# Products ordered by weight tile: all high parts of a tile first, then all its low parts

## The chip, the cores and the metric

The kernel runs on one core of a Trainium2 chip. The metric is the device time of one execution in microseconds; a time stands for the median of several runs. PE is TensorE, DVE is VectorE, ACT is ScalarE, POOL is GpSimd and SP is SyncE, which issues the weight transfers. PEld is TensorE loading the stationary operand of a product, which it does beside the products.

## The reference

A decoder trunk of two layers on a sequence of 256 rows and 1024 channels, in float32. In each layer:

```
h = rmsnorm(x);  p = h @ w_in                      # 1024 x 5888
y_a = short_conv(...) @ w_a_out                    # three mixers on parts of p
y_b = (silu(g) * retention(q, k, v)) @ w_b_out
y_c = spatial_gating(gelu(z)) @ w_c_out
x += (g_a*y_a + g_b*y_b + g_c*y_c) @ w_o           # g_*: sigmoid gates from p
x += cross_attention(rmsnorm(x), rmsnorm(mem))     # xa_q, xa_k, xa_v, xa_o
h = rmsnorm(x)
x += (silu(h @ w1) * (h @ w3)) @ w2                # 1024 -> 2816 -> 1024
```

## The kernel before

**Splitting.** Every float32 weight and activation is split into a high part (rounded to the matmul's float32r) and a low part (the rest). A product of two such numbers is taken as high x high + high x low + low x high.

**The weight stream.** All weights lie in one stream of 128x1024 tiles in the order of use, 320 tiles. `fetch` loads one tile (`raw`, five buffers, an SP DMA), ACT copies it to `hi` (L106), and DVE subtracts to get `lo` (L67), four buffers each. `weights(cols)` hands out the next columns of the current tile.

**Four kinds of chunk.** `chunk_T` makes a transposed result of 256 output channels: for each k of 128 input channels it takes 256 columns of weights; each half of 128 columns is the stationary operand of a 512-column product (`hi` with both parts of x) and of a 256-column product (`lo` with the high part of x). One k is thus two pairs of a 512 and a 256, a chunk of eight k has 32 products, and a tile feeds four k. `chunk_N` (z, g, attention values xv) has the activations stationary and 512 or 256 weight columns moving: for each block of 128 rows high x `hi`, low x `hi`, high x `lo`. `chunk_pair` does two such chunks (qk and v) side by side, one weight tile per k: twelve products of 512. `chunk_y` (branch outputs y, and the last two chunks of w2) multiplies 256 columns each time. The names in the trace are those of the result tiles: gt (gates, 12 chunks a layer), f (w1 and w3, 22 chunks), w (w2), wo, k, q, xv, xo (attention), ax, ac, ab (convolution inputs), and s, pT, av, o, sc, vm, qkT, rT, suT for small products between.

**What sets the order.** TensorE's instructions stand in the order of the program: `InOrder` chains them. The other engines' order is made by the framework's scheduler from a simulated timeline, so it can change when TensorE's order does; each engine then works strictly in its order.

**Accumulators.** `chunk_T`, `chunk_N` and `chunk_pair` share two PSUM buffers (tag mm), so a chunk can begin only when the one two before it has been read: by `summed` (an ACT copy L190 and a DVE add, written `ev<-...`), by `residual` (two DVE adds, `xT<-...`), or by ACT copies (for qk, L331, `mixb<-qk`). Hooks place small products (norm sums, scores, transposes) ahead of a certain k inside a chunk.

In the gates of each layer the memory rows `m` are loaded, scaled on POOL and split by ACT and DVE into `mmt` (lines 454 to 464).

Of the kernel before, what the change touches and what calls it, by code (L numbers as in the profile page):

```python
# [11 lines left out]
F32 = mybir.dt.float32  # L12
# [5 lines left out]
P = 128  # L18
# [3 lines left out]
KT = D // P  # L22
# [3 lines left out]
TW = 1024  # L26
# [28 lines left out]
def decoder_trunk(ctx: ExitStack, tc: tile.TileContext, a, out):  # L55
    nc = tc.nc
    V, A, G, T = nc.vector, nc.scalar, nc.gpsimd, InOrder(tc, nc.tensor)
# [5 lines left out]
    psm = ctx.enter_context(tc.tile_pool(name="psm", bufs=2, space=bass.MemoryType.PSUM))  # L63
# [25 lines left out]
    state = dict(pos=0, loaded=0)  # L89
# [3 lines left out]
    def fetch():  # L93
        n = state["loaded"]
        if n == tiles:
            return
        state["loaded"] = n + 1
        raw = wts.tile([P, TW], F32, tag="raw", name=f"raw{n}", bufs=5)
        hi = wts.tile([P, TW], F32R, tag="hi", name=f"hi{n}", bufs=4)
        lo = wts.tile([P, TW], F32R, tag="lo", name=f"lo{n}", bufs=4)  # L100
        for at, c, m in pieces[n]:
            nc.sync.dma_start(raw[:, at:at + m], ws[c // TW, :, c % TW:c % TW + m])
        w = TW if n else TW // 2
        for c in range(0, TW, w):
            sl = slice(c, c + w)
            A.activation(hi[:, sl], raw[:, sl], AF.Copy)  # L106
            tt(V, lo[:, sl], raw[:, sl], f32(hi[:, sl]), ALU.subtract)
        if n >= 4 and later:
            later.pop(0)()
        ready.append((hi, lo))  # L110

    def weights(cols):
        pos = state["pos"]
        while state["loaded"] <= min(pos // TW + AHEAD, tiles - 1):
            fetch()
        o = pos % TW
        state["pos"] = pos + cols
        hi, lo = ready[pos // TW]
        return hi[:, o:o + cols], lo[:, o:o + cols]


    def chunk_T(xs, kt, name, hooks=None, ps=None, ks=None):


        if ps is None:
            ps = psm.tile([P, 2, 2, S], F32, tag="mm", name=name)
        for k in ks or range(kt):
            if hooks and k in hooks:
                hooks[k]()
            wh, wl = weights(2 * P)  # L130
            x = xs(k)
            for i in range(2):
                c = slice(i * P, (i + 1) * P)
                T.matmul(ps[:, i].rearrange("p t s -> p (t s)"), wh[:, c], x.rearrange("p t s -> p (t s)"),
                         start=(k == 0), stop=False, skip_group_check=True)
                T.matmul(ps[:, i, 1], wl[:, c], x[:, 0], start=False, stop=(k == kt - 1), skip_group_check=True)
        return ps

    def chunk_N(xs, name, hooks=None, n=512):

        ps = psm.tile([P, 2, 512], F32, tag="mm", name=name)
        for k in range(KT):
            if hooks and k in hooks:
                hooks[k]()
            wh, wl = weights(n)
            x = xs(k)
            for b in range(2):
                sl = slice(b * P, (b + 1) * P)
                T.matmul(ps[:, b, 0:n], x[:, 0, sl], wh, start=(k == 0), stop=False)
                T.matmul(ps[:, b, 0:n], x[:, 1, sl], wh, start=False, stop=False)  # L150
                T.matmul(ps[:, b, 0:n], x[:, 0, sl], wl, start=False, stop=(k == KT - 1))
        return ps[:, :, 0:n]

    def chunk_pair(xs, names, hooks):

        pair = [psm.tile([P, 2, 512], F32, tag="mm", name=name) for name in names]
        for k in range(KT):
            if k in hooks:
                hooks[k]()
            x = xs(k)  # L160
            for ps in pair:
                wh, wl = weights(512)
                for b in range(2):
                    sl = slice(b * P, (b + 1) * P)
                    T.matmul(ps[:, b], x[:, 0, sl], wh, start=(k == 0), stop=False)
                    T.matmul(ps[:, b], x[:, 1, sl], wh, start=False, stop=False)
                    T.matmul(ps[:, b], x[:, 0, sl], wl, start=False, stop=(k == KT - 1))
        return pair

    def chunk_y(xs, kt, name, n=2):  # L170

        ps = pss.tile([P, 2, S], F32, tag="sm", name=name)
        for k in range(kt):
            wh, wl = weights(n * P)
            x = xs(k)
            for i in range(n):
                c = slice(i * P, (i + 1) * P)
                T.matmul(ps[:, i], wh[:, c], x[:, 0], start=(k == 0 and i == 0), stop=False, skip_group_check=True)
                T.matmul(ps[:, i], wh[:, c], x[:, 1], start=False, stop=False, skip_group_check=True)
                T.matmul(ps[:, i], wl[:, c], x[:, 0], start=False, stop=(k == kt - 1 and i == n - 1),  # L180
                         skip_group_check=True)
        return ps

    def of(t, k0=0):
        return lambda k: t[:, k0 + k]

    def summed(ps):

        t = wrk.tile([P, 2, S], F32, tag="ev", name="ev", bufs=4)
        A.activation(t, ps[:, :, 1], AF.Copy)  # L190
        tt(V, t, ps[:, :, 0], t, ALU.add)
        return t
# [13 lines left out]
    xs = res.tile([P, KT, 2, S], F32R, name="xs")  # L206
# [83 lines left out]
    def transposes(src, f, name):  # L290

        ps = pss.tile([P, 2, S], F32, tag="sm", name=f"{name}{f}")
        for i in range(2):
            for b in range(2):
                T.transpose(ps[:, i, b * P:(b + 1) * P], src[:, b, (f + i) * P:(f + i + 1) * P], ident)
        return ps
# [9 lines left out]
    for l in range(L):  # L306
# [5 lines left out]
        def pair(x):  # L312
            return x.rearrange("p b (h d) -> p b h d", h=8)
# [6 lines left out]
        def mix_rows():  # L320
            nrm["rb"] = rows_kept(nrm["rn"], f"rb_mix{l}")

        qk, vv = chunk_pair(of(xs), (f"qk{l}", f"v{l}"), {6: mix_cols, 7: mix_rows})
        rn, rb = nrm["rn"], nrm["rb"]
        r2 = wrk.tile([P, S], F32, tag="r2", name=f"r2{l}", bufs=1)
# [3 lines left out]
        t, ra, rbb = pair(mb[:, 0:2]), pair(mb[:, 2:4]), pair(mb[:, 4:6])  # L329
# [8 lines left out]
        for b in range(2):  # L338
            A.activation(vs[:, b], vv[:, b], AF.Copy, scale=rn[:, b:b + 1])

        zz = chunk_N(of(xs), f"z{l}")
        zt = mb[:, 8:10]
        for b in range(2):
# [17 lines left out]
        tt(G, vn, vn, mid(sgg[:, l], 2), ALU.mult)  # L361

        gg = chunk_N(of(xs), f"g{l}")
        sg = mm_[:, 5:7]
        for b in range(2):
# [5 lines left out]


        tx = summed(chunk_T(of(xs), KT, f"ax{l}"))


        scT = mm_[:, 2:5].rearrange("p i s -> p (i s)").rearrange("p (h s) -> p h s", h=4)
        for h in range(4):
            ps = pss.tile([P, 512], F32, tag="sm", name=f"sc{l}_{h}")
# [12 lines left out]
        for g in range(4):  # L391
            sl = slice(g * 64, (g + 1) * 64)
# [3 lines left out]
        G.memset(zp[:, :, 0:2], 0.0)  # L396
        tt(G, tx, tx, mid(r2, 2), ALU.mult)
        tc_ = summed(chunk_T(of(xs), KT, f"ac{l}"))
        tt(G, zp[:, :, 2:], tc_, tx, ALU.mult)
        yc = mb[:, 5].rearrange("p (i s) -> p i s", i=2)  # L400
# [12 lines left out]
        for b in range(2):  # L413
            ps = pss.tile([P, 512], F32, tag="sm", name=f"o{l}_{b}")
# [11 lines left out]
        for b in range(2):  # L426
            for h in range(4):
                i = 4 * b + h
# [3 lines left out]
            tt(G, rv, rv, sg[:, b], ALU.mult)  # L432

        tb = summed(chunk_T(of(xs), KT, f"ab{l}"))
        tt(G, tb, tb, mid(rb, 2), ALU.mult)
        tt(G, yc, yc, tb, ALU.mult)
# [5 lines left out]
        for c in range(12):  # L442
            t = summed(chunk_T(of(xs), KT, f"gt{l}_{c}"))
# [21 lines left out]
            if c == 1:  # L465
                for i in range(2):
                    ps = transposes(rr.rearrange("p b h d -> p b (h d)"), 2 * i, f"rT{l}")
# [6 lines left out]
        for c in range(4):  # L474
            ev = []
            for br, (k0, kn) in enumerate(((0, 2), (2, 4), (6, 2))):
                ps = chunk_y(of(mo, k0), kn, f"y{l}_{c}_{br}")
# [60 lines left out]
        def values(c, n, hooks):  # L538
            ps = chunk_N(of(mmt), f"xv{l}_{c}", hooks, n)
            A.activation(vt[:, :, 0, c:c + n], ps, AF.Copy)  # L540
            tt(V, vt[:, :, 1, c:c + n], ps, f32(vt[:, :, 0, c:c + n]), ALU.subtract)
# [32 lines left out]
        for j in range(4):  # L574
            if j < 2:
                ps = chunk_T(of(ox), KT, f"xo{l}_{j}", ps=xo[j], ks=range(4, KT))
            else:
                ps = chunk_T(of(ox), KT, f"xo{l}_{j}")
# [22 lines left out]
        hooks = {2: {0: ffn_cols}, 3: {0: ffn_rows}}  # L601
        ts = []
        part = [chunk_T(of(xs), KT, f"f{l}_{c}", ks=range(0, KT - 2)) for c in range(2)]
        for c in range(FT):
            if c < 2:
                ps = chunk_T(of(xs), KT, f"f{l}_{c}", ps=part[c], ks=range(KT - 2, KT))
            else:
                ps = chunk_T(of(xs), KT, f"f{l}_{c}", hooks=hooks.get(c))
# [20 lines left out]
    for n in (6, 7):  # L629
        ps = chunk_y(hidden, FT, f"w2_{n}", 1)  # L630
# [100 lines left out]
```

## Time and profile before

| | |
|---|---|
| median of three runs | 968.9 us (968.84 to 968.98) |
| the profiled execution | 969.4 us |
| its span, first to last instruction | 967.6 us |
| mean granted TensorE clock over the span | 0.995 |
| PE busy | 951.8 us (98%) |
| DVE, ACT busy | 713.7 us (74%), 539.8 us (56%) |

The profiled execution is 0.5 us above the median, and 1.8 us of it lie outside the span. Matmuls overlap, so PE being busy 98% of the span says only that it seldom stands still; how fast it goes is read from the starts of its products.

### The profile page before, as it was taken

How to read it: one execution, taken by the hardware profiler on the slowest of the kernel's cores; microseconds unless marked ns; L12 is line 12 of the kernel's file. 1: busy time of each engine (PE TensorE's matmuls, PEld its weight loads, DVE VectorE, ACT ScalarE, POOL GpSimd, SP SyncE). 2: the span in 40 equal slices, each digit the busy share in tenths (PEclk: the TensorE clock that was granted, in tenths of full speed). 3: DMA queues.
4: the chain of work that ended last, by engine and by line, in shares of the span. 5: the costliest groups of instructions: out<-in, count | busy, mean ns of one | idle time of the engine just before them, and what ended most of it. 6: DMA issues, size and time to landing. Idle time of an engine off the chain costs nothing.

```text
span 967.6 us, 14606 instructions
## 1 busy us (share of the span) xinstructions
PE 951.8 (98%) x5622; PEld 836.8 (86%) x5622; DVE 713.7 (74%) x884; ACT 539.8 (56%) x740; POOL 296.1 (31%) x232
## 2 busy tenths in 40 slices
PE   8999999999999999999999989999999999999996
PEld 6788889888998888888888878998889888888886
DVE  7679789886768866657655896799776778666654
ACT  6565765565645755654456465545665466656431
POOL 5943021320114644432134230024100345444211
PEclk9999999999999999999999999999999999999998
DMA  9664665555546565555656355555644556556541
GB/s 310 245 228 145 192 203 186 190 182 170 172 133 194 177 198 191 193 187 180 197 179 194 111 180 193 195 179 172 196 153 151 154 187 191 187 194 194 180 151 44
DMA packets 52630, 175.53 MB, mean 181 GB/s; under 512 B 6096, under 2 KB 6608, under 8 KB 52560
## 3 DMA queue, kind: packets, MB, share of 16 engines
q1 hardware_dynamic: 52128, 174.03, 55.9%
q8 instruction: 44, 0.72, 0.3%
q10 hardware_dynamic: 432, 0.57, 0.2%
q14 instruction: 26, 0.21, 0.1%
HBM read 173.53 MB, written 1.05 MB: 180 GB/s over the span
## 4 chain that ended last, share of the span: by engine, by line
PE 96%; DVE 2%; DMA 1%; issue 0%; SPq 0%; ACT 0%; DVEq 0%
PE f L43 25%; PE gt L43 14%; PE w L43 13%; PE y L43 5%; PE k L43 5%; PE xo L43 5%; PE wo L43 5%; PE xv L43 5%; PE q L43 5%; PE z L43 2%; PE g L43 2%; PE v L43 2%; PE qk L43 2%; PE av L43 1%; PE ac L43 1%; PE s L43 1%
## 5 line engine op out<-in xcount | busy, mean ns | idle before, releaser
L67 DVE TENSOR_TENSOR lo<-raw,hi 128x1024 fp32r<-128x1024 f32 (+1 forms) x321 | 436.8, 1363 | 200.0 <-ACT hi L106 198.0
L106 ACT ACTIVATE hi<-raw 128x1024 fp32r<-128x1024 f32 (+1 forms) x321 | 338.9, 1057 | 315.1 <-issue 67.5
L43 PE MATMUL f<-xs,hi 128*128 128x512 f32 x704 | 245.2, 393 | 0.0
L43 PE MATMUL f<-xs,lo 128*128 128x256 f32 x704 | 196.1, 279 | 0.0
L43 PEld LDWEIGHTS f<-xs,hi 128*128 128x128 f32 x704 | 131.9, 187 | 30.1 <-issue 0.4
L43 PE MATMUL gt<-xs,hi 128*128 128x512 f32 x384 | 136.5, 400 | 2.8 <-DVE ev L67 2.7
L43 PEld LDWEIGHTS f<-xs,lo 128*128 128x128 f32 x704 | 132.6, 188 | 0.0
L67 POOL TENSOR_TENSOR sq<-xT 128x512 f32<-128x512 f32 x27 | 45.8, 1695 | 239.3 <-DVE xT L67 234.5
L43 PE MATMUL gt<-xs,lo 128*128 128x256 f32 x384 | 107.8, 281 | 0.0
L67 POOL TENSOR_TENSOR ev<-ev,rb_ffn 128x512 f32<-128x512 f32 x44 | 63.8, 1453 | 108.3 <-DVE ev L67 85.3
L43 PEld LDWEIGHTS gt<-xs,hi 128*128 128x128 f32 x384 | 72.7, 189 | 20.6 <-DVE ev L67 4.0
L43 PEld LDWEIGHTS gt<-xs,lo 128*128 128x128 f32 x384 | 73.2, 191 | 0.0
L43 PE MATMUL w<-aB,hi 128*128 128x512 f32 (+1 forms) x198 | 62.7, 372 | 0.0
L43 PE MATMUL w<-aA,hi 128*128 128x512 f32 (+1 forms) x198 | 62.3, 371 | 0.0
L67 POOL TENSOR_TENSOR ev<-ev 128x256 f32<-128x256 f32 x44 | 50.5, 1151 | 20.1 <-ACT ev L597 20.1
L202 DVE SCALAR_TENSOR_TENSOR xs<-xT,par,xs 128x256 fp32r<-128x256 f32 x48 | 49.1, 1062 | 4.2 <-ACT xs L201 4.2
L43 PE MATMUL w<-aB,lo 128*128 128x256 f32 x176 | 49.5, 281 | 0.0
L43 PE MATMUL w<-aA,lo 128*128 128x256 f32 x176 | 49.4, 281 | 0.0
L43 PE MATMUL y<-mo,hi 128*128 128x256 f32 x256 | 46.1, 283 | 0.0
L43 PE MATMUL k<-mmt,hi 128*128 128x512 f32 x128 | 45.6, 400 | 0.0
L43 PE MATMUL q<-xs,hi 128*128 128x512 f32 x128 | 45.5, 398 | 0.0
L43 PE MATMUL xo<-ox,hi 128*128 128x512 f32 x128 | 45.4, 399 | 0.0
(251 smaller groups left out, 1779.9 us busy)
## 6 DMA issues: line engine op xcount, KB each, us to landing
raw<-in_ws SPq DMA_DIRECT2D x304, 512.0 KB, 3.5
raw<-in_ws SPq DMA_DIRECT2D x32, 256.0 KB, 4.0
m<-in_memT SPq DMA_DIRECT2D x12, 256.0 KB, 4.0
xT<-in_xT SPq DMA_DIRECT2D x4, 256.0 KB, 5.2
dec<-in_dec SPq DMA_DIRECT2D x1, 512.0 KB, 6.0
wm<-in_wsT SPq DMA_DIRECT2D x2, 256.0 KB, 4.8
out<-xT ACTq DMA_DIRECT2D x2, 256.0 KB, 2.3
sgg<-in_sgg SPq DMA_DIRECT2D x1, 256.0 KB, 5.1
```

The costliest lines, as they stand in the source:

```text
L43: ins = getattr(self.engine, name)(*args, **kwargs)
L67: e.tensor_tensor(o, x, y, op=op)
L106: A.activation(hi[:, sl], raw[:, sl], AF.Copy)
L202: V.scalar_tensor_tensor(lo, x, scale, f32(hi), ALU.mult, ALU.subtract)
```

## The change

Within each weight tile (or the part of it that lies between two hooks or chunk ends) all products with `hi` are issued first, and then all with `lo`. In `chunk_T` a full tile becomes eight products of 512 columns and then eight of 256, where the two alternated. In `chunk_pair` it becomes eight products with `hi` (qk four, v four) and four with `lo` (qk two, v two). The products, their operands, the number of weight loads and the weight stream stay. The core of the diff (`chunk_y` is changed in the same way):

```diff
+    def by_tile(ks, cols, hooks=None):
+        group = []
+        for k in ks:
+            hook = hooks.get(k) if hooks else None
+            if group and (hook or state["pos"] % TW == 0):
+                yield group
+                group = []
+            if hook:
+                hook()
+            group.append((k, *weights(cols)))
+        yield group
...
-        for k in ks or range(kt):
-            if hooks and k in hooks:
-                hooks[k]()
-            wh, wl = weights(2 * P)
-            x = xs(k)
-            for i in range(2):
-                c = slice(i * P, (i + 1) * P)
-                T.matmul(ps[:, i].rearrange("p t s -> p (t s)"), wh[:, c], x.rearrange("p t s -> p (t s)"),
-                         start=(k == 0), stop=False, skip_group_check=True)
-                T.matmul(ps[:, i, 1], wl[:, c], x[:, 0], start=False, stop=(k == kt - 1), skip_group_check=True)
+        for group in by_tile(ks or range(kt), 2 * P, hooks):
+            for k, wh, _ in group:
+                for i in range(2):
+                    T.matmul(ps[:, i].rearrange("p t s -> p (t s)"), wh[:, i * P:(i + 1) * P],
+                             xs(k).rearrange("p t s -> p (t s)"), start=(k == 0), stop=False, skip_group_check=True)
+            for k, _, wl in group:
+                for i in range(2):
+                    T.matmul(ps[:, i, 1], wl[:, i * P:(i + 1) * P], xs(k)[:, 0],
+                             start=False, stop=(k == kt - 1), skip_group_check=True)
...
+    def products_N(group, x):
+        blocks = [slice(b * P, (b + 1) * P) for b in range(2)]
+        for p, k, wh, _ in group:
+            for b in range(2):
+                T.matmul(p[:, b], x(k)[:, 0, blocks[b]], wh, start=(k == 0), stop=False)
+                T.matmul(p[:, b], x(k)[:, 1, blocks[b]], wh, start=False, stop=False)
+        for p, k, _, wl in group:
+            for b in range(2):
+                T.matmul(p[:, b], x(k)[:, 0, blocks[b]], wl, start=False, stop=(k == KT - 1))
...
-            for ps in pair:
-                wh, wl = weights(512)
-                for b in range(2):
-                    sl = slice(b * P, (b + 1) * P)
-                    T.matmul(ps[:, b], x[:, 0, sl], wh, start=(k == 0), stop=False)
-                    T.matmul(ps[:, b], x[:, 1, sl], wh, start=False, stop=False)
-                    T.matmul(ps[:, b], x[:, 0, sl], wl, start=False, stop=(k == KT - 1))
+            products_N([(ps, k, *weights(512)) for ps in pair], xs)
```

The change moves rows on the other engines too. On PE, at the end of the first layer's `chunk_pair` (the eighth k, tiles hi_281 and lo_282) and the beginning of z, stood:

```order
L43 MATMUL rb_mix_ps<-ident,rn_mix_273 128x128 x2
L43 MATMUL qk_172<-hi_281,xs 128x512 x2
L43 MATMUL qk_172<-lo_282,xs 128x512
L43 MATMUL qk_172<-hi_281,xs 128x512 x2
L43 MATMUL qk_172<-lo_282,xs 128x512
L43 MATMUL v_173<-hi_281,xs 128x512 x2
L43 MATMUL v_173<-lo_282,xs 128x512
L43 MATMUL v_173<-hi_281,xs 128x512 x2
L43 MATMUL v_173<-lo_282,xs 128x512
L43 MATMUL z_338<-hi_306,xs 128x512 x2
```

Now there stands, at the same place:

```order
L43 MATMUL rb_mix_ps<-ident,rn_mix_273 128x128 x2
L43 MATMUL qk_172<-hi_281,xs 128x512 x4
L43 MATMUL v_173<-hi_281,xs 128x512 x4
L43 MATMUL qk_172<-lo_282,xs 128x512 x2
L43 MATMUL v_173<-lo_282,xs 128x512 x2
L43 MATMUL z_338<-hi_306,xs 128x512 x8
```

The last product of qk moved from six places ahead of the end to two, and the first of v from the seventh place to the fifth.

On DVE, at the end of the first layer, `residual` of the last w2 chunk (w_3) stood with both its adds together, ahead of the first products of the second layer's v, which take its accumulator:

```order
L67 TENSOR_TENSOR lo_4691<-raw_4689,hi_4690 128x1024
L67 TENSOR_TENSOR lo_4710<-raw_4708,hi_4709 128x1024
L67 TENSOR_TENSOR xT<-w_3_4554,xT 128x512 x2
L67 TENSOR_TENSOR lo_4729<-raw_4727,hi_4728 128x1024
L202 SCALAR_TENSOR_TENSOR xs<-xT,par,xs 128x256 x2
```

Now:

```order
L67 TENSOR_TENSOR lo_4691<-raw_4689,hi_4690 128x1024
L67 TENSOR_TENSOR lo_4710<-raw_4708,hi_4709 128x1024
L67 TENSOR_TENSOR xT<-w_3_4554,xT 128x512
L67 TENSOR_TENSOR lo_4729<-raw_4727,hi_4728 128x1024
L67 TENSOR_TENSOR xT<-w_3_4554,xT 128x512
L214 SCALAR_TENSOR_TENSOR xs<-xT,par,xs 128x256 x2
```

The low part of a weight tile moved in between the two adds.

On DVE, in the second layer's retention (o_0 and o_1 are its outputs in PSUM, st, mv and rs the statistics, zp the convolution's input, mixb its result), from the statistics to the convolution, stood:

```order
L67 TENSOR_TENSOR lo_5251<-raw_5249,hi_5250 128x1024
L422 BN_STATS st_5181<-o_0_5184 128x6 x4
L67 TENSOR_TENSOR lo_5289<-raw_5287,hi_5288 128x1024
L423 BN_AGGR mv_5182<-st_5181 128x2 x2
L67 TENSOR_TENSOR ev<-ac_5126,ev 128x512
L423 BN_AGGR mv_5182<-st_5181 128x2 x2
L422 BN_STATS st_5181<-o_1_5197 128x6 x4
L423 BN_AGGR mv_5182<-st_5181 128x2 x4
L403 TENSOR_SCALAR mixb_4684<-zp,par 128x256 x2
L425 RECIPROCAL rs_5183<-rs_5183 128x8
L404 SCALAR_TENSOR_TENSOR mixb_4684<-zp,par,mixb_4684 128x256 x2
L429 TENSOR_SCALAR mixb_4684<-o_0_5184,mv_5182,rs_5183 128x128 x4
```

Now:

```order
L67 TENSOR_TENSOR lo_5289<-raw_5287,hi_5288 128x1024
L67 TENSOR_TENSOR ev<-ac_5126,ev 128x512
L434 BN_STATS st_5181<-o_0_5184 128x6 x4
L435 BN_AGGR mv_5182<-st_5181 128x2 x2
L434 BN_STATS st_5181<-o_1_5197 128x6 x2
L435 BN_AGGR mv_5182<-st_5181 128x2
L434 BN_STATS st_5181<-o_1_5197 128x6 x2
L435 BN_AGGR mv_5182<-st_5181 128x2 x2
L415 TENSOR_SCALAR mixb_4684<-zp,par 128x256 x2
L435 BN_AGGR mv_5182<-st_5181 128x2 x3
L416 SCALAR_TENSOR_TENSOR mixb_4684<-zp,par,mixb_4684 128x256 x2
L417 SCALAR_TENSOR_TENSOR mixb_4684<-zp,par,mixb_4684 128x256
```

One `lo` and the add for ac moved ahead of the statistics, and the convolution's later passes (L405 before, L417 now) ahead of the normalization (L429). Further on, in the gates, ACT and DVE have two `mmt` splits, which wait for POOL, ahead of the evacuation of a gate chunk where they followed it: the ninth chunk of layer 1 and the second of layer 2. In ffn, `ev<-f` stands behind one more small split on both engines, and at several other residuals a `lo` stands between the two adds.

## Rows read from the trace of the kernel before

**Rows 1.** The page, busy time of each engine: us, share of the span, instructions.
```profile
PE 951.8 (98%) x5622; PEld 836.8 (86%) x5622; DVE 713.7 (74%) x884; ACT 539.8 (56%) x740; POOL 296.1 (31%) x232
```

**Rows 2.** Waits of PE, longest in total first: engine, line, releaser, us, times, longest.
```profile
PE gt L43 <- DVE ev L67: 2.7, 3, 2.1
```

**Rows 3.** The chain that ended last: start us, us, engine, tile, matmuls.
```profile
44.05 10.89 PE g L43 x48
...
147.36 23.03 PE y L43 x192
...
176.04 22.62 PE wo L43 x128
...
419.81 62.10 PE w L43 x352
...
542.08 2.68 PE o L43 x24
...
706.27 1.41 PE s L43 x12
...
790.38 105.39 PE f L43 x608
```

**Rows 4.** Timeline of the first 33 us, PE then ACT: start, us, instruction, wait.
```profile
17.62 0.50 PE L43 MATMUL qk<-lo,xs 128*128 128x512 f32 x1 [0.72 <-DVE lo L67]
...
31.11 0.39 PE L43 MATMUL qk<-lo,xs 128*128 128x512 f32 x1
...
32.87 0.73 PE L43 MATMUL z<-hi,xs 128*128 128x512 f32 x2
...
31.55 1.27 ACT L331 ACTIVATE mixb<-qk,rn_mix 128x512 f32<-128x512 f32 x2
```

**Rows 5.** Timeline where layer 2 begins, PE then DVE.
```profile
481.73 0.63 PE L43 MATMUL qk<-hi,xs 128*128 128x512 f32 x2
...
483.50 0.70 PE L43 MATMUL v<-hi,xs 128*128 128x512 f32 x2 [0.22 <-DVE xT L67]
...
481.93 1.42 DVE L67 TENSOR_TENSOR xT<-w,xT 128x512 f32<-128x512 f32 x2 [0.63 <-PE w L43]
...
483.27 1.22 DVE L67 TENSOR_TENSOR lo<-raw,hi 128x1024 fp32r<-128x1024 f32 x1
```

**Rows 6.** Timeline of layer 2 from retention to the gates, DVE, ACT, PE.
```profile
547.87 0.83 DVE L404 SCALAR_TENSOR_TENSOR mixb<-zp,par,mixb 128x256 f32<-128x256 f32 x2
...
550.53 1.16 DVE L405 SCALAR_TENSOR_TENSOR mixb<-zp,par,mixb 128x256 f32<-128x256 f32 x1
...
553.39 1.51 DVE L405 SCALAR_TENSOR_TENSOR mixb<-zp,par,mixb 128x256 f32<-128x256 f32 x1
...
576.45 0.68 DVE L67 TENSOR_TENSOR ev<-gt,ev 128x512 f32<-128x512 f32 x1
...
568.13 0.91 ACT L201 ACTIVATE mmt<-m,par 128x256 fp32r<-128x256 f32 x2 [3.69 <-POOL m L67]
...
574.80 0.28 PE L43 MATMUL gt<-xs,lo 128*128 128x256 f32 x1
...
577.19 0.50 PE L43 MATMUL gt<-xs,hi 128*128 128x512 f32 x1 [2.11 <-DVE ev L67]
```

**Rows 7.** Windows, core 0: us, PE busy (matmuls), granted clock, DMA share.
```profile
577.00:582.00 5.00, 4.81 (x18) 0.66 0.73 222
```

**Rows 8.** Timeline of layer 1 at the ninth gate chunk, ACT then PE.
```profile
133.91 0.58 ACT L190 ACTIVATE ev<-gt 128x512 f32<-128x512 f32 x1
...
134.39 0.90 ACT L201 ACTIVATE mmt<-m,par 128x256 fp32r<-128x256 f32 x2
...
136.10 0.39 PE L43 MATMUL gt<-xs,hi 128*128 128x512 f32 x1
```

**Rows 9.** Timeline of one ffn chunk, DVE then PE.
```profile
825.82 0.68 DVE L67 TENSOR_TENSOR ev<-f,ev 128x512 f32<-128x512 f32 x1
...
829.05 0.39 PE L43 MATMUL f<-xs,hi 128*128 128x512 f32 x1
```

More of the change, by code (lines that the diff above doesn't have):

```diff
@@ L137, in chunk_T @@
-        return ps
-    def chunk_N(xs, name, hooks=None, n=512):
[L141 to L146, printed above, removed]
-            for b in range(2):
-                sl = slice(b * P, (b + 1) * P)
[L149 to L152, printed above, removed]
+        for group in by_tile(ks or range(kt), 2 * P, hooks):
[7 more added lines that the diff above has]
+                             start=False, stop=(k == kt - 1), skip_group_check=True)
@@ L154, in chunk_pair @@
+    def chunk_N(xs, name, hooks=None, n=512):
+        ps = psm.tile([P, 2, 512], F32, tag="mm", name=name)[:, :, 0:n]
+        for group in by_tile(range(KT), n, hooks):
+            products_N([(ps, *g) for g in group], xs)
+        return ps
     def chunk_pair(xs, names, hooks):
@@ L159, in chunk_pair @@
                 hooks[k]()
-            x = xs(k)
-            for ps in pair:
-                wh, wl = weights(512)
-                for b in range(2):
-                    sl = slice(b * P, (b + 1) * P)
-                    T.matmul(ps[:, b], x[:, 0, sl], wh, start=(k == 0), stop=False)
-                    T.matmul(ps[:, b], x[:, 1, sl], wh, start=False, stop=False)
-                    T.matmul(ps[:, b], x[:, 0, sl], wl, start=False, stop=(k == KT - 1))
+            products_N([(ps, k, *weights(512)) for ps in pair], xs)
         return pair
@@ L172, in chunk_y @@
         ps = pss.tile([P, 2, S], F32, tag="sm", name=name)
[L173 to L181, printed above, removed]
+        for group in by_tile(range(kt), n * P):
+            for k, wh, _ in group:
+                for i in range(n):
+                    c = slice(i * P, (i + 1) * P)
+                    T.matmul(ps[:, i], wh[:, c], xs(k)[:, 0], start=(k == 0 and i == 0), stop=False,
+                             skip_group_check=True)
+                    T.matmul(ps[:, i], wh[:, c], xs(k)[:, 1], start=False, stop=False, skip_group_check=True)
+            for k, _, wl in group:
+                for i in range(n):
+                    c = slice(i * P, (i + 1) * P)
+                    T.matmul(ps[:, i], wl[:, c], xs(k)[:, 0], start=False, stop=(k == kt - 1 and i == n - 1),
+                             skip_group_check=True)
         return ps
```

## Prediction, made before the changed kernel was timed

> **What bounds the kernel now.** I read the page first: PE is busy 951.8 of 967.6 us [rows 1]. Its waits for other engines are few: the largest, gates waiting for the DVE add that frees an accumulator, is 2.7 us in three waits, one of them 2.1 [rows 2]. So time is gained or lost in how closely products follow each other, and in a few stalls. Then I read the chain that ended last, since it gives start, length and count of each stretch of products, and divided [rows 3]:
>
> - g, 512 columns after 512: 10.89 us for 48, 226.9 ns each.
> - y, 256 after 256: 23.03 us for 192, 119.9 ns each. The run of twelve in s: 1.41 us, 117.5 ns each.
> - o, 128 columns: 2.68 us for 24, 111.7 ns each, though half as wide as y: here the product is not what sets the pace.
> - alternating 512 and 256 in `chunk_T`: f 105.39 us for 304 pairs, 346.7 ns a pair; wo 22.62 us for 64 pairs, 353.4; w 62.10 us for 176 pairs, 352.8.
>
> The reader is to see two paces for the same work. f keeps the sum of the two unmixed paces (226.9 + 119.9 = 346.8); wo and w are 6.5 ns slower. Other stretches of the chain, read the same way, put gates, ax and ab with f, and k, xo, ac and most of q with wo. That is about 1,150 pairs at 346.7 and 850 at 353.2, of 2,004.
>
> **The change part by part.**
>
> *Pace of `chunk_T`.* Nothing is added or removed: 4,008 products and as many weight loads. What the order gives is runs of eight of a width. The trace of before has no `chunk_T` run, so I bound its pair from the unmixed rows: below by 226.9 + 117.5 = 344.4, above by 226.9 + 119.9 = 346.8. The first saves 850 x 8.8 + 1,150 x 2.3 = 10.1 us, the second 850 x 6.4 = 5.4 us. A run of eight is nearer in length to s than to y, but it carries on through the whole stage, so I take 345.6: 850 x 7.6 + 1,150 x 1.1 = 7.7 us, **-7.7**.
>
> The Trainium skill (TensorE: Matmul & The Clock Gate, section "Back-to-back issue gap") gives 2.5 ns beyond the columns at 2.4 GHz. By it a 512 would take 215.8 ns and a 256 109.2, and a pair 325 in either order; the 226.9 and 119.9 of the rows do not agree, and they decide. By the rule this term would be 0.
>
> *The start.* In the first tiles PE waits for `lo`, at 17.62 for 0.72 us [rows 4]. This is the third product of a tile's twelve, so ten are still to come; with `lo` last, four are. DVE's order is unchanged there, so `lo` comes when it came. 6 x 0.227 = **-1.4**; at most the wait of the two tiles before it is added (-2), at least nothing if the next tile's data then bind.
>
> *qk's accumulator.* z takes it, and needs both ACT copies of qk. Last product of qk 31.11, copies 31.55 and 1.27 us long, z at 32.87: 1.76 us from one to the other [rows 4]. Before, six products of v (1.36 us and the last of qk, 0.23) covered all but 0.17. Now two of v follow, so with its own 0.227 the cover is 0.68, and z waits 1.08: 0.91 more a layer, **+1.8**. Behind z on PE stands everything.
>
> *v's accumulator in layer 2.* It is w_3's. DVE adds twice from 481.93 for 1.42, and v starts at 483.50 [rows 5]. Now v is wanted two products earlier and a `lo` of 1.22 stands between the adds, so v can start at about 484.5. From there eight products remain of the tile, not six: 484.5 + 1.82 = 486.3 against 483.50 + 1.46 = 484.96, **+1.4** (0.5 if the scheduler's `lo` is somehow done before, 2 if its `hi` is late; what queues behind it on DVE are the `xs` of the last two k, wanted some 16 us later).
>
> *Gate chunks.* Two of the three waits of [rows 2] are short, 0.6 together and 0.1 each for the first product after. They come from DVE being late with ab's add behind retention. In that section a `lo` of 1.22 now stands earlier, and the two convolution passes that took 1.16 and 1.51, where another two took 0.83 together [rows 6], stand ahead of the normalization that feeds POOL; against this the add for ac (0.7, and it waits for its ACT copy) comes first; I give 1.3 us back for it. Net 1.2 + 1.8 - 1.3: about 1.7 us earlier. Both short waits go: **-0.8**.
>
> The long one: the fifth chunk of layer 2 starts at 577.19, 2.39 after the last product of the fourth (0.12 of it that product's own) [rows 6], so 2.27. In the 5 us from 577 the granted clock is 0.66 [rows 7]: PE falls from its 2.4 GHz level to 1.2 after the stall, 0.34 x 5 = 1.7 us more. The chain behind it is `mmt`: ACT is held 3.69 us by POOL until 568.13, then everything behind it is late, the DVE add at 576.45 included. This chain begins in the section above, so it too comes about 1.7 us earlier; the add is done at about 575.4, the chunk wanted at 574.5: a stall of 1.0, after which I take the clock to hold. **-3.0.** Bounds: nothing left (-4.0); or, if DVE is not earlier, the second chunk's evacuation, now behind `mmt`, ends at about 570.7 and stalls the fourth chunk by 1.6, the fifth then by 2 and the clock falls: +2.5.
>
> In layer 1 the ninth chunk's evacuation stood ahead of two `mmt` (0.90 on ACT) and now behind them: 133.91 becomes 134.9, its DVE add ends near 136.7, and the eleventh chunk is wanted at 136.10 [rows 8]. **+0.6** (0 to 1).
>
> *At nothing:* the reordered `ev<-f` is about 0.4 us later, covered by the distance from its add (825.82, 0.68 long) to the next use of that accumulator, which is later than 829.05 [rows 9]; without this cover it would cost 0.4 in each of 44 chunks. The `lo` between the adds of wo, xo and w costs 1.2 us of a chunk's 5.5, and only at v is the next chunk that near. z, g, xv and y keep one width, so the order cannot change their pace.
>
> Sum: -7.7 - 1.4 + 1.8 + 1.4 - 0.8 - 3.0 + 0.6 = -9.1. From the profiled execution's 969.4 this is 960.3; that run is 0.5 above the median, so **959.8 us**.
>
> **The rivals.**
>
> *A: the order does not change the pace.* The 353 is then a property of those stages and not of alternating. For it: f and wo alternate alike, and f is at 346.7. Against: stages at 353 share no engine's load with each other (w has little DVE work, q much). The rest of the sum, -1.4, stays: 967.5. The Trainium skill (the same page and section) ends here too, since its gap has only columns in it; its prices enter nothing here.
>
> *B: the gate stall stays or grows* (its upper bound above, with the pace gained). For it: `mmt` now stands ahead of an evacuation. Against: DVE's section before it is shorter. 959.8 + 3.0 to + 5.5: 963 to 965.
>
> *C, slower: the 512-column runs keep the wide spacing.* In the slow stages the 512 takes about 353 - 118 = 235 before its successor starts; if that comes from weight loads that lag behind (the 128-column products at 111.7 [rows 3] show that something beside the columns takes that long), a run of eight narrow products at 119.9 leaves the loads late for the next wide run, and all 2,004 pairs would be 355. That is 850 x 1.8 + 1,150 x 8.3 = +11.1 in place of -7.7: 978.6. It turns into a loss where a pair passes about 350.2 (mean of before 349.5, and 1.4 us from the rest over 2,004). Against: g's 226.9 is a run in which each product has its own weight load.
>
> *D: the runs reach s's pace and no gate stall is left:* 959.8 - 2.4 - 1.0 = 956.4.
>
> **How the numbers follow.** Forecast 0.55 (957.5 to 962), B 0.20, A 0.09, D 0.10, C 0.06. A measurement of this kernel tells 0.2% (1.9 us) from no change. Faster by more than that, below 967.0: forecast, B, D and a small part of A, 0.87. Within it: most of A, 0.07. Slower: C, 0.06. The range takes D in and reaches past B nearly to A: 955.5 to 966.
>
> **What would show it.** In the changed trace: f, gt, k and w all at one pace, near 345.6 ns a pair, with no stage at 353; z starting about 1.1 us after the last product of v in both layers; v of layer 2 waiting some 1.8 us for the second add of w_3; no wait for ab's add; a gate stall in layer 2 of about 1 us and no window of lower clock behind it. It is wrong if a run of 256 goes slower than 122 ns or one of 512 slower than 229, if a stall I count as short drops the clock (1.7 us each), or if the DVE order, which I follow by hand, starves the gates.

## The result and the profile after

The change makes the kernel slower: 975.15 us, median of four runs (974.69 to 975.28), against 968.94 (968.84 to 970.17) for the kernel before beside it; ratio 1.0057, 95% interval 1.0045 to 1.0070. The loss is small, about half a per cent. The profiled execution took 975.26 us with a span of 973.5, 5.9 more than before. I had predicted 959.8.

The page after, busy time of each engine, for [rows 1]:

```profile
PE 953.8 (98%) x5622; PEld 839.8 (86%) x5622; DVE 682.4 (70%) x884; ACT 532.2 (55%) x740; POOL 310.6 (32%) x232
```

DVE is busy 31 us less and POOL 14.5 more, though the numbers of their instructions are the same. This is the first sign that the loss has to do with them. The waits of PE, for [rows 2]:

```profile
PE z L43 <- ACT mixb L343: 2.3, 2, 1.4
PE v L43 <- DVE xT L67: 1.7, 1, 1.7
PE gt L43 <- DVE ev L67: 1.5, 2, 1.3
...
PE vm L43 <- DVE mixm L67: 1.0, 2, 0.5
```

They show z, v and vm, but no wait in f: the stalls there, shown next, do not appear in this list. The chain that ended last, where [rows 3] had one unbroken piece of f, 105.39 us for 608 products:

```profile
655.81 22.35 PE wo L43 x128
...
787.61 5.70 PE f L43 x32
793.52 61.73 PE f L43 x352
855.27 5.85 PE f L43 x32
861.15 5.86 PE f L43 x32
...
896.44 5.87 PE f L43 x32
```

The chain now breaks at each chunk from 855 on, and a chunk takes 5.87 us where the 352 products ahead of it take 61.73 / 11 = 5.61. wo is at 22.35 / 64 = 349.2 ns a pair (353.4 in [rows 3]).

Where the time went: from the start of the first product of each stretch to that of the next (the last stretch ends with w), how much longer (+) it takes than in the trace of before, in us. Two later kernels, explained below, stand beside it.

| stretch, to the start of the next | after | evac_first | snake |
|---|---|---|---|
| start, qk and v, layer 1 | +1.05 | +1.22 | +0.65 |
| z to ab, layer 1 | +0.45 | +0.47 | +0.63 |
| gates, layer 1 | -0.31 | -0.31 | -0.43 |
| y to xo, layer 1 | -0.81 | -0.83 | -1.09 |
| f, layer 1 | **+3.62** | +0.88 | +0.44 |
| w, layer 1 | -0.68 | -0.81 | -0.88 |
| qk and v, layer 2 | **+2.66** | +2.66 | -0.03 |
| z to ab, layer 2 | +0.47 | +0.48 | +0.63 |
| gates, layer 2 | -2.70 | -2.69 | -4.91 |
| y to xo, layer 2 | -0.84 | -0.84 | -1.11 |
| f, layer 2 | **+3.81** | +0.97 | +0.55 |
| w, layer 2 | -0.62 | -0.71 | -0.76 |
| sum | +6.10 | +0.49 | -6.31 |

**The ffn in the changed trace.** Timeline of one chunk of layer 1, ACT, then DVE, then POOL (start, us, instruction, wait before it):

```profile
396.49 0.42 ACT L609 ACTIVATE ev<-ev 128x256 f32<-128x256 f32 x1 [2.76 <-POOL ev L67]
396.82 1.04 ACT L106 ACTIVATE hi<-raw 128x1024 fp32r<-128x1024 f32 x1
397.77 0.41 ACT L210 ACTIVATE aB<-ev 128x256 fp32r<-128x256 f32 x1
398.08 0.58 ACT L202 ACTIVATE ev<-f 128x512 f32<-128x512 f32 x1
...
394.09 1.22 DVE L67 TENSOR_TENSOR lo<-raw,hi 128x1024 fp32r<-128x1024 f32 x1
397.89 1.23 DVE L67 TENSOR_TENSOR lo<-raw,hi 128x1024 fp32r<-128x1024 f32 x1 [2.59 <-ACT hi L106]
399.04 0.42 DVE L67 TENSOR_TENSOR aB<-ev,aB 128x256 fp32r<-128x256 f32 x1
399.37 0.68 DVE L67 TENSOR_TENSOR ev<-f,ev 128x512 f32<-128x512 f32 x1
...
394.25 2.21 POOL L67 TENSOR_TENSOR ev<-ev,rb_ffn 128x512 f32<-128x512 f32 x1 [2.40 <-DVE ev L67]
400.14 2.21 POOL L67 TENSOR_TENSOR ev<-ev,rb_ffn 128x512 f32<-128x512 f32 x1 [2.41 <-DVE ev L67]
```

This is a closed loop. POOL's product of `ev` and `rb_ffn` (394.25) releases the Silu on ACT (396.49); the weights' hi copy stands behind it; DVE's `lo` waits for that copy (397.89); behind `lo` stand the split of aB and the add of the next `ev<-f` (399.37), and that add releases POOL again (400.14). No instruction in it waits for PE. One turn is 400.14 - 394.25 = 5.89 us, a chunk of PE at the grouped pace 16 x 349.2 ns = 5.59. The accumulators are freed 0.29 us later in each chunk; the slack of some 3 us, [rows 9], lasts about eleven chunks, and then PE runs at the pace of the loop.

In the kernel before the same stretch of layer 1 read, ACT, then DVE, then POOL:

```profile
394.76 1.06 ACT L106 ACTIVATE hi<-raw 128x1024 fp32r<-128x1024 f32 x1 [0.93 <-PE f L43]
...
394.23 0.68 DVE L67 TENSOR_TENSOR ev<-f,ev 128x512 f32<-128x512 f32 x1
394.83 0.41 DVE L67 TENSOR_TENSOR aB<-ev,aB 128x256 fp32r<-128x256 f32 x1
395.86 1.62 DVE L67 TENSOR_TENSOR lo<-raw,hi 128x1024 fp32r<-128x1024 f32 x1 [0.61 <-ACT hi L106]
...
394.99 1.41 POOL L67 TENSOR_TENSOR ev<-ev,rb_ffn 128x512 f32<-128x512 f32 x1 [2.46 <-DVE ev L67]
```

There the add stood ahead of the split of aB, POOL took 1.41 us, and ACT's copy waited for PE: PE set the pace.

### The profile page after: what moved, and what is told of

Its sections match the earlier page's. It is cut to its first block, busy times and chain, and to the rows that moved or that the text cites. A ratio compares the mean times of both kernels' runs of the same rounds, so it can differ in the third digit from the quotient of the medians.

```text
span 973.5 us, 14604 instructions
## 1 busy us (share of the span) xinstructions
PE 953.8 (98%) x5622; PEld 839.8 (86%) x5622; DVE 682.4 (70%) x884; ACT 532.2 (55%) x740; POOL 310.6 (32%) x232
## 3 DMA queue, kind: packets, MB, share of 16 engines
HBM read 173.53 MB, written 1.05 MB: 179 GB/s over the span
## 5 line engine op out<-in xcount | busy, mean ns | idle before, releaser
L67 DVE TENSOR_TENSOR lo<-raw,hi 128x1024 fp32r<-128x1024 f32 (+1 forms) x321 | 414.2, 1293 | 229.2 <-ACT hi L106 223.7
L43 PE MATMUL f<-xs,hi 128*128 128x512 f32 x704 | 179.7, 396 | 0.5
L67 POOL TENSOR_TENSOR ev<-ev,rb_ffn 128x512 f32<-128x512 f32 x44 | 92.4, 2105 | 107.4 <-DVE ev L67 86.1
L43 PEld LDWEIGHTS f<-xs,lo 128*128 128x128 f32 x704 | 96.5, 190 | 7.4
L43 PE MATMUL f<-xs,lo 128*128 128x256 f32 x704 | 98.6, 282 | 0.0
L43 PE MATMUL gt<-xs,hi 128*128 128x512 f32 x384 | 96.9, 394 | 1.5 <-DVE ev L67 1.5
L43 PEld LDWEIGHTS gt<-xs,lo 128*128 128x128 f32 x384 | 52.4, 190 | 3.8
L43 PE MATMUL gt<-xs,lo 128*128 128x256 f32 x384 | 53.5, 282 | 0.0
L43 PEld LDWEIGHTS w<-aB,hi 128*128 128x128 f32 x198 | 33.3, 189 | 5.1
L43 PEld LDWEIGHTS w<-aA,hi 128*128 128x128 f32 x198 | 32.5, 188 | 5.2 <-DVE ev L67 0.4
```

What stands on the lines that cost most here:

```text
L43: ins = getattr(self.engine, name)(*args, **kwargs)
L67: e.tensor_tensor(o, x, y, op=op)
```

## Experiments

In every comparison below, the kernel before ran beside the others on the same chip. Its runs there lie between 968.2 and 975.5 us, with medians of 970.9 to 971.1 over 17 to 29 runs, some 2 us above the median of four in the result; why they spread is itself a result (below).

**evac_first: the order of ACT and DVE in the ffn, alone.** The products stay grouped.

```diff
-            split(hidden(c), t[:, 0])
+            h = hidden(c)
+            behind(A.activation(h[:, 0], t[:, 0], AF.Copy), last["A"])
+            behind(V.tensor_tensor(h[:, 1], t[:, 0], f32(h[:, 0]), op=ALU.subtract), last["V"])
```

`behind` only orders two instructions of one engine; `last` holds the ACT copy and the DVE add of the latest `summed`. 

> The changed kernel with one constraint on ACT and DVE: in the ffn the split of a gated chunk (aA, aB) stands behind the evacuation of the next chunk (ev<-f), as it stood before the change; the product order is the changed one. Theory L (a closed loop): in the changed trace the loop DVE add, POOL product with rb_ffn 2.2 us, Silu, hi copy, split, ev<-f takes 5.88 us, more than a chunk of 5.59, and costs 0.29 us in about 19 chunks. Then this kernel has no stall at the chunk starts of f, and its time is 975.2 - 5.5 = 969.7 us (969 to 970.5). Rival P (the stalls belong to the grouped products themselves): the stalls of about 0.18 us at the chunk starts stay and the time is 974.5 to 975.5.

Measured: 969.66 us (969.31 to 971.68, 12 runs), ratio 0.9984 (0.9974 to 0.9995). The stalls of f are gone; its chain has one piece again, at 106.16 / 304 = 349.2 ns a pair, and POOL's product is back from a mean of 2,105 ns to 1,453. Chain and groups of evac_first:

```profile
790.82 106.16 PE f L43 x608
...
L67 POOL TENSOR_TENSOR ev<-ev,rb_ffn 128x512 f32<-128x512 f32 x44 | 63.8, 1453 | 107.5 <-DVE ev L212 86.1 <-ACT rb_ffn L293 21.3
```

Theory L holds: the loss in f came from the order on ACT and DVE, which followed from the products' order, and not from the grouped products themselves. Which of the two constraints did it was not tested apart.

**f_alt: the products of f alternate, the rest is grouped** (in `chunk_T`, names that begin with f take the old order). 

> The changed kernel with the products of f alternating as before, all other chunks grouped. Theory L: the order of ACT and DVE in the ffn is that of before again, so the 5.5 us of stalls go, and the pairs of f go from 349.2 to 346.7 ns, 640 x 2.5 = 1.6 us: 975.2 - 7.1 = 968.1 us (967.3 to 969). Rival Q (grouped and alternating f have the same pace and only the stalls count): 969.7. Rival P predicts 968 too, and is told apart by the first kernel.

Measured: 970.96 us (967.64 to 972.64), ratio 1.0001 (0.9987 to 1.0015). The stalls are gone, as expected, but the time is a miss: neither 968.1 nor steady. The chain of f_alt, layer 2:

```profile
790.09 107.42 PE f L43 x608
```

That is 353.4 ns a pair, where the same products in the same order had 346.7 in [rows 3]. In layer 1 of the same execution the last 608 products of f went at 347.0 (first start 314.87, first of w 420.35). So the two paces that I had read as belonging to stages do not: f can have either.

**f_only: the kernel before, with only f grouped** (and the branch products y, whose products have one width). 

> The kernel before with the products of f grouped and nothing else changed. Theory L: the loop of 5.88 us appears in the ffn, the f pairs go from 346.7 to 349.2: 968.9 + 5.5 + 1.6 = 976.0 us (975 to 977), more than the whole change. What is left of the change, outside f, is then a gain of about 0.9 us. Rival (the loss sits at the accumulators of z and v and in the start): 969 to 970.

Measured: 976.88 us (976.02 to 977.56), ratio 1.0060 (1.0042 to 1.0078). The loop appears with nothing else changed (its turn is 5.88 us at the same place, and POOL's product has a mean of 2,103 ns), and this part alone costs as much as the whole change.

**pair_alt: `chunk_pair` alternates, all else grouped.** 

> The changed kernel with chunk_pair (qk and v) alternating as before, all else grouped. Theory: the waits of z for the copies of qk (1.07 and 1.61 us beyond the pace, before 0.16 and 0.14) and of v in layer 2 (1.85, before 0.38) go, -2.4 and -1.5: 975.2 - 3.9 = 971.3 us (970.5 to 972.3). Rival (an equal wait appears elsewhere, as at rb_mix and in layer 2's rows, since the first products are then later again): 974 to 975.5.

Measured: 972.96 us (972.73 to 973.69), ratio 1.0022 (1.0011 to 1.0034); 2.35 below the changed kernel in after_again (975.31, on another chip) and above the range expected. z no longer waits; v of layer 2 still does:

```profile
PE v L43 <- DVE xT L67: 1.2, 1, 1.2
```

I had given all of v's wait to the product order. The larger part belongs to DVE's order, which this kernel keeps; its timeline at v has `lo` between the two adds of w_3:

```profile
484.52 0.69 DVE L67 TENSOR_TENSOR xT<-w,xT 128x512 f32<-128x512 f32 x1 [1.43 <-PE w L43]
485.13 1.22 DVE L67 TENSOR_TENSOR lo<-raw,hi 128x1024 fp32r<-128x1024 f32 x1
486.26 0.69 DVE L67 TENSOR_TENSOR xT<-w,xT 128x512 f32<-128x512 f32 x1
```

**after_again.** 

> The changed kernel once more, on the chip of the other runs of this call. All theories: 975 us, 0.6% above the kernel before. Theory S (alternating products settle into one of two spacings, 346.7 or 353 ns a pair, at each interruption, by chance; grouped ones always take 349.2) expects its runs to lie within 1 us, while those of the kernel before spread over some 5 us. Rival (a stage has its own pace): both spread alike.

Measured: 975.31 us (975.24 to 976.0), ratio 1.0049 (1.0032 to 1.0067). Its seven runs lie within 0.8 us; the 21 of the kernel before beside it between 968.61 and 975.47. That is what theory S expects, and not its rival.

**before_again and before_third: the kernel before, unchanged.** 

> The kernel before, unchanged, with a profile of its own. Theory S (each stretch of alternating products falls into 346.7 or 353 ns a pair by chance, at interruptions): some stretches of this execution stand in the other spacing than in the profile of before, f, gt, w or q by layer, and the time differs by 3.2 us for each 500 pairs that changed; the runs spread over some 5 us. Rival (each stage has its own pace): the stages show the paces of the first profile, f 346.7 in both layers, wo, xo and w 353.

> The same program once more: theory S expects other stretches to have changed than in before_again; the rival expects the same paces a third time.

Measured: 971.17 us (969.8 to 974.27; ratio 1.0002, 0.9988 to 1.0016) and 969.2. The chain of before_again, ac and f of each layer and wo:

```profile
64.91 5.55 PE ac L43 x32
...
177.37 22.61 PE wo L43 x128
...
315.53 107.42 PE f L43 x608
...
539.50 5.65 PE ac L43 x32
...
792.38 105.39 PE f L43 x608
```

f of layer 1 went at 353.4 ns a pair, f of layer 2 at 346.7; ac at 5.55 us in one layer and 5.65 in the other. In before_third f is at 105.39 in both layers:

```profile
315.50 105.39 PE f L43 x608
...
790.41 105.39 PE f L43 x608
```

So one program shows either spacing in one stage, for hundreds of products without a change. Not everything flips: wo, xo, w and all but the last 12 pairs of k stood near 353 in all three executions; f, gt, ac, ab and q did not stay. Both theories are half right, and one f block is worth 107.42 - 105.39 = 2.03 us. What picks the spacing stays open; in these traces it changes only where the stream is interrupted (a stall, a few narrow products). The granted clock does not make the spread: at one mean clock, 0.996, the nine such runs of the kernel before beside evac_first lie between 968.98 and 973.14. In f_alt, where only f alternates, the runs still spread over 5.0 us.

**evac_pair: both mends together** (evac_first and pair_alt). 

> The changed kernel with both mends: evacuation ahead of the split in the ffn, and chunk_pair alternating. If the two costs add: 975.2 - 5.5 - 2.2 = 967.5 us (966.7 to 968.3), with v of layer 2 still waiting 1.4 us. Rival (one takes the other's cover): 969 to 970.

Measured: 967.59 us (966.83 to 968.12), ratio 0.9959 (0.9943 to 0.9975). The two add.

**snake: evac_pair, and in `chunk_T` every second tile begins with its low part.**

```diff
-        for group in by_tile(ks or range(kt), 2 * P, hooks):
...
+        for g, group in enumerate(by_tile(ks or range(kt), 2 * P, hooks)):
+            for part in ("hi", "lo") if g % 2 == 0 else ("lo", "hi"):
```

> As evac_pair, but in the transposed chunks every second tile begins with its low part (high, low, low, high), so that there is one change from 256 to 512 columns in two tiles. Theory T (the grouped pair of 349.2 is 346.7 plus about 20 ns at each change from narrow to wide): 348.0 ns a pair, 2,004 x 1.2 = 2.4 us less than evac_pair, about 965. Rival (the grouped pace is a fixed mean, as a third spacing): 349.2 a pair and the time of evac_pair. The order of ACT and DVE differs from evac_pair's, so the pace is read from the spacings of the trace.

Measured: 962.67 us (962.34 to 963.03), ratio 0.9917 (0.9897 to 0.9937). Timeline of PE in f, first of the changed kernel:

```profile
351.02 2.00 PE L43 MATMUL f<-xs,hi 128*128 128x512 f32 x8
352.87 1.11 PE L43 MATMUL f<-xs,lo 128*128 128x256 f32 x8
353.82 2.00 PE L43 MATMUL f<-xs,hi 128*128 128x512 f32 x8
```

and then of snake:

```profile
351.20 3.82 PE L43 MATMUL f<-xs,hi 128*128 128x512 f32 x16
354.85 2.08 PE L43 MATMUL f<-xs,lo 128*128 128x256 f32 x16
356.76 0.63 PE L43 MATMUL f<-xs,hi 128*128 128x512 f32 x2
```

The starts give eight wide products in 1.85 us, 231 each, and sixteen in 3.65, 228 each. f takes 105.78 us:

```profile
314.22 105.78 PE f L43 x608
```

That is 348.0 ns a pair, as theory T says. Theory T gives 2.4 of the 4.9 us to evac_pair. The other 2.5 I put down to DVE's order, which is another here, by the traces and not by a run of its own: the two adds of w_3 stand together again (v waits 0.2 and not 1.2), and no gate chunk waits (1.5 in evac_pair); vm waits 0.4 longer:

```profile
PE vm L43 <- DVE mixm L67: 1.3, 2, 0.6
...
PE v L43 <- DVE xT L67: 0.2, 1, 0.2
```

**runs2: runs of two.** 

> As evac_pair, but the transposed chunks group within one k only: two products of 512, then two of 256, so four changes from narrow to wide in a tile. Theory T: wide spacings stay at the 236 and 229 ns with which a wide run begins, narrow ones at 118.8, a pair of 351.3 ns: 4.2 us more than evac_pair, about 971.7. Rival (fixed mean): 349.2 and no change.

Measured: 966.5 us (965.69 to 968.26), ratio 0.9958 (0.9942 to 0.9974). A miss for theory T as I put it, and for its rival:

```profile
314.02 105.90 PE f L43 x608
```

348.4 ns a pair, not 351.3 or 349.2. The starts of single products in f of layer 1 show why. In snake, after a change to wide come 233, 236, 229, 232, 231 ns and then 227; after a change to narrow 113, 119 and then 120. In runs2 the wide ones pay (233 mean) but both narrow ones are of the quick kind (115 mean):

```profile
350.79 0.63 PE L43 MATMUL f<-xs,hi 128*128 128x512 f32 x2
351.26 0.39 PE L43 MATMUL f<-xs,lo 128*128 128x256 f32 x2
351.49 0.63 PE L43 MATMUL f<-xs,hi 128*128 128x512 f32 x2
```

I had counted the loss and not the gain. Its total is under evac_pair's by 1.1. Beside the pace it has another DVE order, with no wait at vm and 0.2 at v, but a longer one in the gates (2.3).

**snake_vm: snake, with the four products vm after the chunk ac.** 

> As snake, with the four products vm issued after the chunk ac and not before it. In snake they wait 0.80 us beyond the pace in each layer, behind the DVE multiplications of sc. If ac covers that wait and nothing takes its place: 962.7 - 1.6 = 961.1 us (960.6 to 961.8). Rival (what follows ac waits for vm's consumers, or another accumulator becomes late): 962.5 to 964.

Measured: 961.27 us (960.83 to 961.74), ratio 0.9900 (0.9881 to 0.9919). The wait at vm is gone and nothing took its place. It is the fastest version, 1.0% under the kernel before and 1.4% under the changed one.

## Why the prediction was wrong

Forecast (-9.1) and change (+6.2) differ by 15 us. Two steps make up 12.4 of it.

**"At nothing: the reordered `ev<-f`" failed.** I had seen the new order and priced it once, 0.4 us against a cover of 3. But it repeats: it closes the loop above, with a turn of 5.89 us against a chunk of 5.59. Cost: the f rows of the table less those of evac_first, 2.74 + 2.84 = 5.6 us. evac_first took 5.65 away (975.31 to 969.66, on two chips where the kernel before had the same median), and f_only brought it into the kernel before. The loop is longer than a chunk only because POOL's product now starts just after a DVE `lo` and takes 2.21 us, not 1.41; with 1.41 the turn would be 5.1 and PE would pace it. This last part is worked out, not tried. The Trainium skill (SBUF — State Buffer, "Who interferes with whom") says that a DVE instruction with two SBUF inputs contends with a GpSimd one that reads SBUF, that their shared port is an exclusive lock, and that the order of issue decides which one waits. The rows agree in direction, both ways: here `lo`, first at 394.09, keeps 1.22 and POOL takes 2.21; in evac_first POOL is first, keeps its 1.41, and the `lo` behind it takes 1.60. If each waited for the full rest of the other, an estimate from these rows is 2.47 and 1.74, so the measured waits are a little shorter than a full lock. The rows of evac_first:

```profile
395.38 1.41 POOL L67 TENSOR_TENSOR ev<-ev,rb_ffn 128x512 f32<-128x512 f32 x1 [2.50 <-DVE ev L212]
...
396.27 1.60 DVE L67 TENSOR_TENSOR lo<-raw,hi 128x1024 fp32r<-128x1024 f32 x1 [0.64 <-ACT hi L106]
```

**The pace, -7.7, was mis-sized: about -0.9.** From the evac_first column: f +1.85; from the column after: y to xo and w -2.95, and gates of layer 1 +0.2 without the 0.48 us of their vanished wait. All stages came to nearly one pace, as forecast, but at 349.2 (w, with its broken tiles, some 0.5 lower) and not 345.6. The sign that I had named came true: a run of eight wide products takes 231 ns each, above 229. Rival C had the place right (a wide run begins with wide spacings) and the size wrong: 20 ns a tile, not every product; that weight loads lag there is not shown. No order ran clearly under the unmixed 346.8 (lowest 346.7, when alternating): the bound from s does not hold, and the 850 pairs at 353 were partly chance, so a share of that gain was not the order's to give.

**The start, -1.4: nothing.** The start to z is +1.05, of which 0.9 is z's wait. What the first tiles gained, the norm's wait gave back (rb_mix_ps 1.4 us, before 0.7). The same stretch differs by 0.77 between two executions of the kernel before, so more cannot be told.

**z and v, +1.8 and +1.4: right, z a little small.** z starts 1.07 and 1.61 us beyond the pace (before 0.16 and 0.14), +2.4; v 1.85 (before 0.38), +1.5. By pair_alt, evac_pair and snake z's belongs to the product order, v's mostly to DVE's.

**Gates, -3.8 in all: -2.7 in layer 2, -0.3 in layer 1.** The short waits went, as forecast. The long one did not shrink to 1.0: it became 1.42 us at the fifth chunk and 0.43 at the fourth, together only 0.4 less than the 2.27 of before. Most of the -2.7 is the clock, which did not fall; in before six pairs at the low clock took 528 to 641 ns in place of 346.7, 1.6 us together. That part was luck (last section). The clock after:

```profile
577.00:582.00 5.00, 3.96 (x25) 3.37 (x24) 4.98 (x8) 5.00 (x9) 0.00 (x0) 1.00 0.24 77
582.00:587.00 5.00, 4.78 (x25) 4.11 (x26) 4.92 (x7) 3.44 (x5) 0.00 (x0) 1.00 0.80 249
```

The ninth chunk's +0.6 in layer 1 did not come.

**Not seen at all:** vm waits 0.43 us more in each layer, for DVE's multiplications of sc, +0.9. snake_vm takes this away.

## What to carry to other kernels

A delay that recurs in every turn of a loop is not priced against the slack of one turn: follow the new order around until it comes back to its first instruction, and compare the turn with the loop that covers it. Where a scheduler orders the other engines, changing one engine's order changes them all, and here that was worth more than the change itself; pinning two instructions gave 5.65 us back. And before a pace is taken for a property of a stage, look at the same stage in a second execution.

## What the hardware showed beyond expectation

- Alternating 512 and 256 products settle at 346.7 or 353.4 ns a pair and stay there up to the next interruption; f took both in the same program. In runs of eight and sixteen the long stages stay near 349.2 and 348.0, and the spread of the kernels' times shrinks with it: 0.8 us in after_again, 1.3 in evac_pair and 0.7 in snake, 7 for the kernel before on the same chip. The widest of the kernels whose f is grouped are evac_first with 2.4, of which one run makes 1.6, and runs2 with 2.6.
- The same stall need not cost the clock. After a wait of 2.11 us at the fifth gate chunk the granted clock fell to 0.66 in the profile of before [rows 7]; after the same wait it held in before_again:

```profile
580.28 0.50 PE L43 MATMUL gt<-xs,hi 128*128 128x512 f32 x1 [2.11 <-DVE ev L67]
...
580.00:585.00 5.00, 4.72 (x27) 1.00 0.83 244
```

It fell to 0.66 again in f_only, and held in before_third and, after 2.3 us, in runs2. So the 1.6 us that the changed kernel gained there over the profile of before was chance, not the change.
